# Norm factors in the input blocks, raw queries asked for two steps ahead, values copied inside DRAM to one block per column group and loaded whole

## The chip, the cores and the metric

The kernel runs on one core of one Trainium2 chip. A core has five engines that run side by side and wait for one another by semaphores: TensorE (PE in the profile; its weight loads are listed apart as PEld), VectorE (DVE), ScalarE (ACT), GpSimd (POOL) and SyncE (SP). Here SP does nothing but issue transfers (DMAs), and nearly all of the kernel's transfers stand in that one queue. TensorE writes its results to PSUM, which has eight banks of 128x512 float32 values, and ACT and DVE read them from there.

The metric is the device time of one execution in microseconds (us); lower is better.

## The reference

`DEPTH` is 1, so only the first layer is computed: 2-D neighbourhood attention with 16 heads of 64 on a grid of 32 rows by 64 columns, a SiLU gate and a residual, between two RMSNorms. Everything is float32.

```python
S, D, H, HD = 2048, 1024, 16, 64                  # 32 rows x 64 columns
h = rmsnorm(x, norm_0)                            # x * rsqrt(mean(x*x) + eps) * norm_0
q, k, v, gate = split(h @ w_in_0, 4)              # (2048 x 1024) @ (1024 x 4096)
for every row r and every block of 16 query columns:
    keys   = 8 rows around r x 32 columns around the block
    s = q @ keys.T / 8 + bias(rpb_0)              # only the 8 x 16 keys of the query's own
    o = softmax(where(valid, s, -1e30)) @ v       #   neighbourhood are valid
x = x + (o * silu(gate)) @ w_out_0
return rmsnorm(x, norm_f)
```

## The kernel before

A float32 product is made of three TensorE passes over operands that are split into a high and a low part: high x high, high x low, low x high. A split takes one ACT copy (the high part) and one DVE subtraction (the low part). `split_to` does this for inputs, `split_q` for queries, `split_og` for the attention's result, `use_item` for weights.

The first RMSNorm is not applied to x before the projection. The factor per feature, `norm_0` (`g0`, read through `gain`), is multiplied in when an input block is split. The factor per token, 1/rms, is computed while the first projections run (`stats`), and multiplied into the projection's result. For q, k and gate, whose results lie features by tokens, it is first spread over the partitions: `diagonal(c)` (four small DVE operations, an ACT copy and a DVE subtraction) and `spread_rstd(c)` (two matmuls, one ACT copy) give `rb[c]`, a 128x512 tile for the 512 tokens of chunk c. `evac` then multiplies a PSUM bank by `rb[c]` on DVE (L326 for k, L328 for q and gate), and `out_` does it on GpSimd (L439). For values, `evac_v` multiplies by a column of `rt` on ACT.

The work runs in three stages.

- `stage_one` (chunks 0 and 1, 1024 tokens): the values, then q, k and gate of all eight head pairs by a scheme of seven block products in place of eight (`seven_products`, a Strassen-Winograd form). Twelve units (four times k, q, g) have seven products each, in the order 1, 6, 2, 7, 5, 4, 3; a product is twelve matmuls of 128x128 by 128x512. Some products add into a bank in which an earlier product still stands until DVE has read it (`add`, `out_`). Operands of coming products are formed six products ahead (`ahead`).
- `stage_two` (chunks 2 and 3): the values of these tokens, then three more units.
- The attention loop, 66 iterations of which 64 have a pair (head pair p, token block T of eight grid rows, half of the four column groups C). Iteration i runs, in this order on TensorE: `feed`, some 20 matmuls of what is left (first `projections`, 36 groups of 24 matmuls for chunks 2 and 3, then `outputs`, the product with `w_out`); `turns(i-2)`, the transposes of the probabilities, which ACT and DVE copy out of PSUM into `pta`; `scores(i)`, then DVE adds bias and mask (L970) and ACT takes the exponentials (L973); `values(i-2)`, probabilities times values. `feed(n, calm)` does not stop within `calm` matmuls of the last evacuation.

All of q, k (high and low part), gate and v pass through DRAM (`qd`, `k_hi`, `k_lo`, `sgd`, `vd`) between projection and attention. `vd` holds the values by grid row (r within a group of four, column c, group g). A value tile `vt` for one column group is loaded by four transfers, one for each r (`load_v`, `rows`, L920), since only then the partitions are contiguous in DRAM; that makes 32 blocks x 4 column groups x 4 transfers.

The order of the work is written out by hand, engine by engine. A clock that counts matmuls (`due`) triggers what `store(key, lag, f)` and `later_loads` have put off by `lag` matmuls. `begin(i)` asks for loads: in an even iteration the keys of the next block (lag 0 and 2), then the biases of a new head pair (4 and 6), the gate (7); in every iteration i > 0 the value tiles of pair i-1 (eight transfers from lag 1 on). `middle(i)`, after 45% of the iteration's feed, splits in even iterations the queries that this same iteration's `scores` need, and asks for the raw queries of the next block. In an even iteration in which p or the kind of block changes, `bias` also puts six operations on GpSimd (L945). `split_og(n)` (two ACT copies and two DVE subtractions, L1103 and L1104) is called from `ahead(k)` inside `outputs`, whenever tile n is due within one turn and was loaded long enough ago, whatever the iteration.

Engines take their instructions strictly in this order, so an instruction that waits holds up everything behind it on its engine. Of a pool with n buffers, the next tile waits until a buffer is released by all who read it.

Of the kernel before, what the change touches and what calls it, by code (L numbers as in the profile page):

```python
# [10 lines left out]
F32 = mybir.dt.float32  # L11
# [59 lines left out]
def build(ctx, tc, x, xr, xt, wg, rpb, w_out, n0, nf, masks, out):  # L71
# [7 lines left out]
    vd = [dram.tile([4, 4, GW, 8, 128], F32, name=f"vd{u}") for u in range(2)]  # L79
    ogd = [dram.tile([128, 4, NP, 128], F32, name=f"ogd{T}") for T in range(4)]  # L80
# [71 lines left out]
    def split_x(a, b, t, tiles=None):  # L152
        h, l = tiles or (xs([128, 512], F32R, "hh"), xs([128, 512], F32R, "hl"))
        hh[a, b], hl[a, b] = h, l
        nc.scalar.activation(h, t, AF.Copy, scale=g0[:, a:a + 1])
        nc.vector.scalar_tensor_tensor(l, t, g0[:, a:a + 1], h.bitcast(F32), op0=OP.mult, op1=OP.subtract)

    def use_item(it):
# [3 lines left out]
        if kind == "x":  # L162
            split_x(a, b, t, (hh[a, b], hl[a, b]))
# [125 lines left out]
    pending = []  # L289
# [23 lines left out]
    def flush(c):  # L313
        if c not in rb:
            if c not in dgs:
                diagonal(c)
            spread_rstd(c)
        for e in [e for e in pending if e[0] == c]:
            pending.remove(e)
            e[1]()  # L320

    def evac(kind, hp, c, p, then=None):
        state["event"] = clock[0]
        tmp = ev([128, 512], F32, "tmp")
        if kind == "k":
            nc.vector.tensor_tensor(tmp, p, rb[c], OP.mult)  # L326
        else:
            nc.vector.tensor_tensor(blocked(tmp), tiled(p), tiled(rb[c]), OP.mult)  # L328
# [5 lines left out]
    def give(kind, hp, c, tmp):  # L334
        while sum(e[1][0] in "kqg" for e in later) > 1:
            later.pop(0)[2]()
        s = slice(c * 512, c * 512 + 512)
        if kind == "g":
            sg = ev([128, 512], F32, "sg")
            nc.scalar.activation(sg, tmp, AF.Tanh, scale=0.5)  # L340
            nc.vector.scalar_tensor_tensor(sg, sg, 1.0, tmp, op0=OP.add, op1=OP.mult)
            written.add(("g", hp, c))
            store(("g", hp, c), 12, lambda: nc.sync.dma_start(sgd[hp][:, s], sg))
            return
        written.add((kind, hp, c))
        if kind == "q":
            store(("q", hp, c), 12, lambda: nc.sync.dma_start(qd[hp][:, s], tmp))
# [3 lines left out]
        nc.scalar.activation(hi, tmp, AF.Copy)  # L351
        nc.vector.tensor_tensor(lo, tmp, hi.bitcast(F32), OP.subtract)
# [22 lines left out]
    def evac_v(u, t, p):  # L375
        v = ev([128, 512], F32, "v")
        nc.scalar.activation(v, p, AF.Copy, scale=rt[:, t:t + 1])
# [10 lines left out]
    def seven_products(us, c0, X1, also):  # L388
# [45 lines left out]
        def out_(n, a, c, P, u, then):  # L434
            kind, j = us[n]
            tmp = ev([128, 512], F32, "tmp")
            lay, of = (lambda t: t, lambda t: t) if kind == "k" else (blocked, tiled)
            nc.vector.tensor_tensor(lay(tmp), of(B[n, P]), of(u), OP.add)  # L438
            nc.gpsimd.tensor_tensor(lay(tmp), lay(tmp), of(rb[c]), OP.mult)  # L439
# [16 lines left out]
        def run():  # L456
            then = []
            for i, (n, P) in enumerate(seq):
# [7 lines left out]
                elif P == 2:  # L466
                    evac(kind, 2 * j, c0, B[n, 2], then)
# [901 lines left out]
```

## Time and profile before

| | us |
|---|---|
| median of 3 runs | 1103.4 (1100.61 to 1104.03) |
| the profiled execution | 1102.79 |
| its span, first to last instruction | 1101.0 |
| PE busy | 1080.7 |
| DVE busy | 732.7 |
| ACT busy | 531.5 |
| POOL busy | 378.5 |

The profile is one execution; its span is 1.8 us shorter than the time that was measured for that same execution. Times in views of the trace count from the span's start. Stage one reaches to about 326 us, stage two to about 462 us, the attention loop to about 1046 us; the rest is the end of the output product.

A row of the view by stretches gives the length of the stretch, then for each engine its busy time and number of instructions, the granted TensorE clock (1.00 is full speed) and the busy share and rate of the DMA engines. A row of the timeline gives start, duration, engine, source line, operation and tiles, and in brackets how long the engine had idled and what ended that. A row of the groups gives line, engine, operation, tiles and shape, count, then total busy time in us and the mean of one in ns.

### The profile page before, as it was taken

To read this page: it belongs to the slowest core of one execution; us is meant where nothing else is said; L and a number is where in the kernel's file an instruction comes from. 1 tells how busy PE (TensorE), PEld (TensorE's weight loads), DVE (VectorE), ACT (ScalarE), POOL (GpSimd) and SP (SyncE) were. 2 spreads that over 40 slices of the span, in tenths; PEclk is the share of its full clock that TensorE was granted. 3 is DMA by queue.
4 is the path that set the end of the run, shared out by engine and by line. 5 is a ranking of instruction groups with operands and counts; after the bars stand their busy time and mean duration, and the time that the engine had idled before them with its cause. 6 is when DMAs were issued, how large, how long until landed. Compare 5 with 4: busy or idle time off the path is not lost.

```text
span 1101.0 us, 22543 instructions
## 1 busy us (share of the span) xinstructions
PE 1080.7 (98%) x7657; PEld 883.6 (80%) x7657; DVE 732.7 (67%) x1663; ACT 531.5 (48%) x1336; POOL 378.5 (34%) x483
## 2 busy tenths in 40 slices
PE   9999999999999999999999999999999999999997
PEld 6888888888888888877888888888877888887885
DVE  5376778788777337575665766665777777776644
ACT  7545343343344433255554554564556555555422
POOL 0000312222130001245445444424447666675200
PEclk9999999999999999998999999999999999999999
DMA  8633545454574235587767878687979797887452
GB/s 307 209 96 105 185 132 181 143 173 112 166 216 138 80 89 157 195 263 232 233 193 241 251 223 230 211 268 222 259 237 286 228 288 225 252 274 211 152 153 77
DMA packets 142962, 217.29 MB, mean 197 GB/s; under 512 B 18048, under 2 KB 65408, under 8 KB 142848
## 3 DMA queue, kind: packets, MB, share of 16 engines
q1 hardware_dynamic: 142704, 215.58, 64.6%
q8 instruction: 62, 1.02, 0.4%
q14 instruction: 52, 0.43, 0.1%
q10 hardware_dynamic: 144, 0.26, 0.1%
HBM read 157.05 MB, written 58.72 MB: 196 GB/s over the span
## 4 chain that ended last, share of the span: by engine, by line
PE 88%; DVE 5%; DMA 3%; issue 2%; ACT 1%; POOL 1%; SPq 0%; DVEq 0%; POOLq 0%
PE pp L421 24%; PE pv L534 16%; PE o L1031 7%; PE s L963 6%; PE pp L369 6%; PE pp L367 6%; PE pp L365 5%; PE po L1227 5%; PE po L1223 4%; PE po L1225 4%; PE ph L986 4%; ACT x L973 1%; PE zp L1242 1%; DVE gl L1104 1%; DMA sgt<-sgd 0%
## 5 line engine op out<-in xcount | busy, mean ns | idle before, releaser
L981 POOL TENSOR_SCALAR x<-x,st 128x360 f32<-128x360 f32 (+5 forms) x256 | 143.1, 579 | 239.1 <-DVE st L979 157.1
L439 POOL TENSOR_TENSOR tmp<-tmp,rb 128x512 f32<-128x512 f32 x45 | 73.5, 1634 | 399.2 <-DVE tmp L438 358.4
L973 ACT ACTIVATE x<-x,st 128x360 f32<-128x360 f32 (+5 forms) x256 | 151.8, 594 | 56.4 <-DVE st L970 56.4
L421 PE MATMUL pp<-h,f 128*128 128x512 f32 x480 | 155.4, 389 | 0.0
L945 POOL TENSOR_TENSOR em<-e,mk 128x480 f32<-128x480 f32 (+5 forms) x160 | 140.8, 915 | 5.0 <-DVE st L970 5.0
L421 PE MATMUL pp<-t,f 128*128 128x512 f32 x540 | 129.8, 389 | 0.1
L970 DVE CUSTOM_DVE_ANT_0 x<-s,em 128x360 f32<-128x360 f32 (+5 forms) x256 | 123.8, 538 | 5.1 <-PE s L963 2.0
L421 PEld LDWEIGHTS pp<-t,f 128*128 128x128 f32 x540 | 101.3, 188 | 21.5 <-DVE u L432 0.6
L369 PE MATMUL pp<-h,w 128*128 128x512 f32 x288 | 115.9, 403 | 0.0
L367 PE MATMUL pp<-l,w 128*128 128x512 f32 x288 | 114.2, 397 | 0.0
L365 PE MATMUL pp<-h,w 128*128 128x512 f32 x288 | 113.6, 394 | 0.0
L1010 ACT ACTIVATE pta<-ph 96x256 f32<-96x256 f32 (+1 forms) x224 | 58.8, 333 | 105.8 <-PE ph L986 105.8
L1031 PEld LDWEIGHTS o<-pta,vt 96*64 96x64 f32 (+2 forms) x1792 | 86.0, 139 | 24.2 <-DVE pta L1011 10.2
L421 PEld LDWEIGHTS pp<-h,f 128*128 128x128 f32 x480 | 90.1, 188 | 18.8
L1031 PE MATMUL o<-pta,vt 96*64 96x128 f32 (+4 forms) x1792 | 95.2, 258 | 7.5 <-DVE pta L1011 4.6
L1227 PE MATMUL po<-wol,gh 128*128 128x512 f32 x252 | 101.4, 403 | 0.0
L1223 PE MATMUL po<-woh,gh 128*128 128x512 f32 x252 | 100.0, 397 | 0.0
L1225 PE MATMUL po<-woh,gl 128*128 128x512 f32 x252 | 99.7, 395 | 0.0
L1011 DVE COPY pta<-ph 128x384 f32<-128x384 f32 (+3 forms) x128 | 60.5, 513 | 51.5 <-PE ph L986 51.2
L421 PE MATMUL pp<-l,f 128*128 128x512 f32 x240 | 93.4, 389 | 0.0
L534 PE MATMUL pv<-wh,h 128*128 128x512 f32 x256 | 88.1, 390 | 0.0
L534 PE MATMUL pv<-wh,l 128*128 128x512 f32 x256 | 88.0, 389 | 0.0
(136 smaller groups left out, 1951.1 us busy)
## 6 DMA issues: line engine op xcount, KB each, us to landing
raw<-in_wg_dram SPq DMA_DIRECT2D x126, 256.0 KB
e<-in_rpb_dram SPq DMA_DIRECT2D x54, 240.0 KB
vt<-vd SPq DMA_DIRECT2D x256, 48.0 KB
row<-in_xr_dram SPq DMA_DIRECT2D x32, 256.0 KB
vd<-v SPq DMA_DIRECT2D x32, 256.0 KB
k_hi<-hi SPq DMA_DIRECT2D x32, 256.0 KB
k_lo<-lo SPq DMA_DIRECT2D x32, 256.0 KB
qd<-tmp SPq DMA_DIRECT2D x32, 256.0 KB
```

What stands on the lines that cost most here:

```text
L365: nc.tensor.matmul(p, wh[w, b][:, cols], hh[k, c], start=(k == 0), stop=False)
L367: nc.tensor.matmul(p, wh[w, b][:, cols], hl[k, c], start=False, stop=False)
L369: nc.tensor.matmul(p, wl[w, b][:, cols], hh[k, c], start=False, stop=(k == NK - 1))
L421: nc.tensor.matmul(B[n, P], t[:, int(m == 2), c], x[k][int(m == 1)], start=P in (1, 6, 5) and k == 0 and m == 0, stop=k == 3 and m == 2, s ...
L534: nc.tensor.matmul(ps[t], a[:, o], b, start=k == 0 and m == 0, stop=k == NK - 1 and m == 2)
L945: (nc.gpsimd if attending[0] or not s else nc.vector).tensor_tensor(sh(t), E[p, s][:, u0 + 4:u1 + 4, v0 + 8:v1 + 8], sh(MK[0][:, m0:m0 + n ...
L973: nc.scalar.activation(X[i, C][s], X[i, C][s], AF.Exp, bias=st[:, s:s + 1], scale=-1.0, accum_out=st[:, 2 + s:3 + s])
L981: nc.gpsimd.tensor_scalar(X[i, C][s], X[i, C][s], st[:, 4 + s:5 + s], 0.5, op0=OP.mult, op1=OP.mult)
L1031: nc.tensor.matmul(o[s * 64:s * 64 + 64, C * 128 + q0:C * 128 + q0 + nq], vt[C][:k, g - g0_, s * 64:s * 64 + 64], t[:k, at:at + nq], start ...
L1223: nc.tensor.matmul(p, gh, woh[q, j], start=(i == 0), stop=False)
L1225: nc.tensor.matmul(p, gl, woh[q, j], start=False, stop=False)
L1227: nc.tensor.matmul(p, gh, wol[q, j], start=False, stop=(i == NK - 1))
```

## The change

1. **Norm factors in the input blocks.** For chunks 2 and 3 both factors are multiplied into the raw input block by one DVE operation (`normed`) before it is split. The results of stage two and of the attention loop's projections then need no `rb`: `evac` (with `flush` and `pending`) is gone from `projections`, `out_` skips GpSimd, and `give` works on the PSUM bank itself (`psum=True`): ACT copies the high part of k, or takes the tanh of the gate, or copies q, and DVE reads the bank for k and gate. `diagonal(2)`, `diagonal(3)` and `spread_rstd(2)` move from stage two into stage one, where four of the input blocks are also loaded and eight are normed earlier; `spread_rstd(3)` moves to the start of stage two. In exchange the gate is stored in plain order and reordered when it is used (L1045).
2. **Raw queries two steps ahead.** The queries of the next block are split in the middle of the odd iteration before (`middle`), and the raw queries of the block after that are asked for there, into the one buffer of pool `lp`.
3. **Values as one block per column group.** 64 transfers inside DRAM (`copy_v`) copy `vd` to `vc[p, C]`: 32 in stage one (three in each unit from the second), 32 in stage two. A value tile is then one transfer (`load_v`).
4. **Order in the attention loop.** The two value transfers of `begin` come first (lag 0 and 2), then new biases (5 and 8), keys (9 and 13), gate (15). `split_og` gets a condition: in odd iterations after the first quarter of the feed (`quiet`) up to two turns ahead, in even ones only in the second half of the turn just before.

```diff
+    vc = {(p, C): dram.tile([4 * (c1 - c0), 8, 128], F32, name=f"vc{p}_{C}")
+          for p in range(NP) for C, (c0, c1) in enumerate(KEY_COLS)}
...
-    def give(kind, hp, c, tmp):
+    def give(kind, hp, c, t, psum=False):
...
+            if psum:
+                o = ev([128, 512], F32, "q")
+                nc.scalar.activation(blocked(o), tiled(t), AF.Copy)
+                t = o
...
-        nc.scalar.activation(hi, tmp, AF.Copy)
-        nc.vector.tensor_tensor(lo, tmp, hi.bitcast(F32), OP.subtract)
+        nc.scalar.activation(hi, t, AF.Copy)
+        nc.vector.tensor_tensor(lo, t, hi.bitcast(F32), OP.subtract)
...
-            nc.gpsimd.tensor_tensor(lay(tmp), lay(tmp), of(rb[c]), OP.mult)
+            if c0 == 0:
+                nc.gpsimd.tensor_tensor(lay(tmp), lay(tmp), of(rb[c]), OP.mult)
...
+    def normed(f, c, k, t):
+        nc.vector.scalar_tensor_tensor(t, t, gain(f, k), rb[c], op0=OP.mult, op1=OP.mult)
...
+            if m and i in (1, 3, 5):
+                copies(0, 1)
...
+            if (n, i) == (-3, 1):
+                diagonal(2)
+            if (n, i) == (-3, 3):
+                spread_rstd(2)
+            if (n, i) == (-3, 4):
+                diagonal(3)
...
+        norms = {(-2, 3): ("x11", 0), (-2, 5): ("x11", 1), (-1, 0): ("x11", 2), (-1, 1): ("x11", 3),
+                 (-1, 3): ("x21", 0), (-1, 4): ("x21", 1), (-1, 5): ("x21", 2), (-1, 6): ("x21", 3)}
...
-                    split_to(*X2[f][k], x[k], gain(f, k))
+                    normed(f, 3, k, x[k])
+                    split_to(*X2[f][k], x[k], None)
...
-                pending.append((c, lambda kind=kind, hp=2 * j + a, c=c, p=p: evac(kind, hp, c, p)))
-                flush(c)
+                state["event"] = clock[0]
+                give(kind, 2 * j + a, c, p, True)
...
-        return [lambda r=r: rows(r) for r in range(4)]
+        def block():
+            VT[p, T, C] = t = vp([128, 4, 128], F32, "vt")
+            nc.sync.dma_start(t[:4 * (c1 - c0), :g1_ - g0_], vc[p, C][:, g0_:g1_])
+
+        return [block]
+
+    def copy_v(p, C, h):
+        must(*[("v", p // 4, t) for t in range(8 * h, 8 * h + 8)])
+        c0, c1 = KEY_COLS[C]
+        g = slice(512 * h, 512 * h + 512)
+        nc.sync.dma_start(vc[p, C].rearrange("(r c) g d -> c r (g d)", r=4)[:, :, g],
+                          vd[p // 4][p % 4].rearrange("r c g d -> c r (g d)")[c0:c1, :, g])
...
-            if n < ready["loaded"] and place[n] <= k + 1 and clock[0] - loaded_at[n] >= 28 and whole(n):
+            near = 2 if quiet[0] else 1 if i >= 4 else 0
+            if n < ready["loaded"] and place[n] <= k + near and clock[0] - loaded_at[n] >= 28 and whole(n):
...
+        if 0 < i <= N:
+            p, T, cs = pairs[i - 1]
+            later_loads(load_v(p, T, cs[0]) + load_v(p, T, cs[1]), 0, 2)
...
-                later_loads([kh, kl], 0, 2)
+                kh, kl = load_k(*nx)
                 if nx[0] != p:
-                    later_loads(load_e(nx[0]), 4, 2)
+                    later_loads(load_e(nx[0]), 5, 3)
+                later_loads([kh, kl], 9, 4)
...
-            later_loads([lambda: load_sg(p, T)], 7, 0)
+            later_loads([lambda: load_sg(p, T)], 15, 0)
...
     def middle(i):
-        if i % 2 or i >= N:
-            return
         m = i // 2
-        if type(QT[order[m]]) is not tuple:
-            split_q(*order[m])
-        if m + 1 < len(order):
-            later_loads([LOADS[m + 1][1]], 1, 0)
+        if i % 2 and m + 1 < len(order):
+            split_q(*order[m + 1])
+        if i == 0 or i % 2 and m + 2 < len(order):
+            later_loads([load_q(*order[m + (2 if i else 1)])], 1, 0)
...
+        quiet[0] = i % 2 == 1 or i >= N
+        feed(a * 0.2)
         middle(i)
         feed(a * 0.55, 8)
+        quiet[0] = i >= N
```

119 lines of the change are left out of this document (54 added, 65 removed).

## The prediction, made before the changed kernel ran

> **What bounds the kernel now.** I read the busy shares first, then the chain of waits for TensorE's pace, then a view by stretches for the places where TensorE falls short of that pace.
>
> ```profile
> span 1101.0 us, 22543 instructions
> PE 1080.7 (98%) x7657; PEld 883.6 (80%) x7657; DVE 732.7 (67%) x1663; ACT 531.5 (48%) x1336; POOL 378.5 (34%) x483
> 97.56 70.73 PE pp L421 x312
> 10.00:462.00 452.00, 451.87 (x1993) 373.68 (x1992) 310.36 (x485) 195.42 (x362) 68.63 (x42) 1.00 0.51 154
> 462.00:486.00 24.00, 24.00 (x117) 19.37 (x117) 17.74 (x30) 10.38 (x23) 8.33 (x7) 1.00 0.89 302
> 486.00:508.00 22.00, 19.02 (x158) 14.97 (x155) 14.34 (x44) 11.59 (x38) 14.77 (x23) 0.84 0.77 229
> 508.00:800.00 292.00, 291.59 (x2829) 237.99 (x2828) 183.95 (x515) 155.11 (x470) 133.58 (x200) 1.00 0.79 234
> 800.00:820.00 20.00, 17.95 (x175) 14.35 (x174) 15.70 (x36) 12.87 (x35) 11.15 (x14) 0.91 0.83 255
> 820.00:845.00 25.00, 23.22 (x251) 19.05 (x250) 19.68 (x48) 14.76 (x43) 14.91 (x20) 0.93 0.82 251
> 845.00:1000.00 155.00, 153.47 (x1518) 125.93 (x1520) 115.50 (x351) 90.46 (x268) 101.40 (x140) 1.00 0.83 252
> 1000.00:1022.00 22.00, 20.36 (x188) 16.64 (x186) 13.92 (x45) 11.80 (x36) 12.38 (x19) 0.92 0.77 231
> 1022.00:1046.00 24.00, 23.68 (x213) 19.27 (x212) 13.73 (x40) 9.48 (x26) 6.98 (x10) 1.00 0.44 133
> ```
>
> TensorE is the bound: busy 1080.7 of 1101.0 us, and 312 matmuls in 70.73 us are 0.227 us each, its pace wherever nothing holds it up. The change adds and removes no matmul, so it can only win what TensorE loses to waits. Up to 462 us that is 0.13 us in 452. In the attention loop each stretch loses its idle time (length minus PE busy) and the part of the clock that was not granted. 486 to 508: 2.98 + 22 x 0.16 = 6.5. 800 to 845: 3.83 + 20 x 0.09 + 25 x 0.07 = 7.4. 1000 to 1022: 1.64 + 22 x 0.08 = 3.4. The rest, 0.41 + 1.53 + 0.32 = 2.3. Together **19.6 us is the ceiling** of any gain; I take the end after 1046 us as unchanged.
>
> What stands behind the three large losses? TensorE's waits and the work that ended them:
>
> ```profile
> 493.68 0.39 PE L963 MATMUL s<-kt,ql 64*128 64x264 f32 x2 [0.25 <-DVE ql L499]
> 495.54 0.43 PE L963 MATMUL s<-kt,qh 64*128 64x352 f32 x1 [1.47 <-DVE tmp L326]
> 497.15 0.95 PE L963 MATMUL s<-kt,qh 64*128 64x352 f32 x3 [1.18 <-ACT pta L1010]
> 492.90 0.72 DVE L499 SCALAR_TENSOR_TENSOR ql<-qr,qh 128x512 fp32r<-128x512 f32 x1 [1.69 <-ACT qh L498]
> 494.80 0.68 DVE L326 TENSOR_TENSOR tmp<-pp,rb 128x512 f32<-128x512 f32 x1
> 805.91 4.72 POOL L945 TENSOR_TENSOR em<-e,mk 128x480 f32<-128x480 f32 x4
> 806.91 1.72 DVE L499 SCALAR_TENSOR_TENSOR ql<-qr,qh 128x512 fp32r<-128x512 f32 x1 [1.13 <-ACT qh L498]
> 808.55 2.63 DVE L1104 TENSOR_TENSOR gl<-ograw,gh 128x512 fp32r<-128x512 f32 x2
> 811.83 1.56 PE L1031 MATMUL o<-pta,vt 96*64 96x128 f32 x32 [2.04 <-DVE pta L1011]
> 814.07 0.43 PE pp L369
> L499 DVE SCALAR_TENSOR_TENSOR ql<-qr,qh x32: 677/708/1825, 473.6 to 1012.4; 128x512 fp32r<-128x512 f32 x32
> L1104 DVE TENSOR_TENSOR gl<-ograw,gh x32: 549/684/1779, 808.6 to 1078.3; 128x512 fp32r<-128x512 f32 x30, 128x384 fp32r<-128x384 f32 x2
> ```
>
> At 493 us ACT reaches the query split only after the exponentials, DVE waits 1.69 us for it, and behind it on DVE stands L326, which alone can free a PSUM bank that the scores need. At 808 us the query split and an output split take 1.72 + 2.63 = 4.35 us of DVE where undisturbed ones (medians 0.708 and 0.684) would take 0.71 + 1.37 = 2.1: GpSimd is working on the bias tiles meanwhile. The copy of the transposes stands behind them. Both are even iterations, and the splits stand just ahead of the work that TensorE waits for. After its wait of 2.04 us TensorE runs at 0.43 us a matmul, half pace.
>
> The Trainium skill, page "TensorE: Matmul & The Clock Gate", section "HAM oscillation — how this bites in real kernels", asks for an idle gap over about 3.4 us before the clock falls. This trace differs: waits of 2.04 us and less were followed by half pace, and the measurement decides. By the page the ceiling would be the idle time alone, 0.13 + 10.7 = 10.8 us.
>
> At 1000 us the wait is for a value tile:
>
> ```profile
> 1005.46 5.86 SPq L920 DMA_DIRECT2D vt<-vd  x10
> 1003.28 4.91 DMA sgt<-sgd
> 1010.88 0.92 PE L1031 MATMUL o<-pta,vt 96*64 96x128 f32 x12 [1.64 <-DMA vt<-vd]
> L920 SPq DMA_DIRECT2D vt<-vd x512: 289/379/1847, 480.2 to 1035.9; - x171
> ```
>
> Ten value transfers occupied SP for 5.86 us, behind keys, queries and the gate.
>
> **The change, part by part.** The prices:
>
> ```profile
> L328 DVE TENSOR_TENSOR tmp<-pp,rb 128x512 f32<-128x512 f32 x34 | 23.4, 689 | 37.1 <-PE pp L369 31.2 <-PE pp L421 5.8
> L439 POOL TENSOR_TENSOR tmp<-tmp,rb 128x512 f32<-128x512 f32 x45 | 73.5, 1634 | 399.2 <-DVE tmp L438 358.4 <-DMA raw<-in_wg_dram 12.9 <-DMA qr<-qd 12.0
> L428 ACT ACTIVATE p<-pp 128x512 f32<-128x512 f32 x15 | 9.0, 598 | 44.4 <-PE pp L421 44.4
> L499 DVE SCALAR_TENSOR_TENSOR l<-spot,g,h 128x512 fp32r<-128x512 f32 x6 | 4.4, 748 | 0.1
> L206 DVE TENSOR_SCALAR dg<-ident,rt 128x128 f32<-128x128 f32 x16 | 3.5, 280 | 0.0
> L210 DVE TENSOR_TENSOR dgl<-dg,dgh 128x512 fp32r<-128x512 f32 x4 | 2.8, 692 | 2.8 <-ACT dgh L209 2.8
> 250.00:269.10 19.10, 19.10 (x86) 15.83 (x85) 16.38 (x32) 5.21 (x9) 5.02 (x4) 1.00 0.41 99
> 288.10:307.10 19.00, 19.00 (x86) 15.73 (x85) 14.72 (x20) 6.37 (x11) 4.84 (x4) 1.00 0.50 166
> q1 hardware_dynamic: 142704, 215.58, 64.6%
> ```
>
> *Norm factors, attention loop.* The 36 groups lose one DVE multiplication each, 36 x 0.689 = 24.8 us of DVE, and the 12 of q gain an ACT copy out of PSUM, 12 x 0.598 = 7.2 us of ACT. None of it is TensorE's; it counts through the waits. The link L326 drops out of the chain at 493 us.
>
> *Norm factors, stages one and two.* Nine GpSimd products go, 9 x 1.634 = 14.7 us, and three on DVE. Added on DVE are 16 products of gain and `rb`; the nearest row is L499 on `spot`, 0.748, so 12.0 us. Eight of them are in stage one, with two diagonals of 4 x 0.280 + 0.692 = 1.8 us. Both diagonals fall in the unit of 250 to 269 us: 16.38 + 3.6 = 20.0 of 19.1 us. The unit of 288 to 307 us gets six products: 14.72 + 4.5 = 19.2 of 19.0. DVE is full there, but TensorE needs a sum only after one product in between, 12 x 0.227 = 2.7 us, and an overrun of 0.9 us stays inside that. Bounds: 0, and 4.0 us if all six products are stretched like the worst split (6 x 1.825 = 11.0): 14.72 + 11.0 - 19.0 = 6.7, less the 2.7 of slack. I take 0.5, nearer to nothing. Over both stages DVE is busy 310 of 452 us, and stage two's blocks are needed only two pairs of token tiles later, so 0 there.
>
> *Copies in DRAM.* 16 half-copies per column group: 2 x 8 x 2 x (192 + 256) KB = 14.7 MB. The queue's own row prices a MB at 64.6% x 1101 / 215.58 = 3.3 us of all 16 engines, so 48 us, and double if a move inside DRAM costs twice. They lie between about 116 and 463 us, 347 us in which the DMA share of 0.51 becomes 0.65 or 0.79. TensorE lost nothing at 0.89 (462 to 486 us). 64 issues of 0.38 us are 24 us of SP. I take 0; the bounds are 0 and 1.
>
> *Queries and output splits.* The query split goes to odd iterations, where no new bias tiles occupy GpSimd, a full iteration ahead of its scores. Output splits leave the even iterations but for the last half of a turn. Behind the split on DVE then stands the evacuation of a group, no longer the scores of the same iteration. Of the 6.5 us at 486 to 508 I take 5.0 (bounds 2.5, half, and 6.5), since the weight splits stay; of the 7.4 at 800 to 845, 6.0 (bounds 3 and 7.4), of the scattered 2.3, 1.2 (0.5 and 2.3).
>
> *Values whole, and first.* 512 issues become 128, so 384 x 0.379 = 146 us of SP go, and the two that a pair needs stand ahead of keys, gate and biases. Late next would be gate or keys, and these have more than half an iteration. Of the 3.4 us at 1000 to 1022 I take 2.8 (bounds 0 and 3.4): landing itself takes a few us (4.91 for the gate).
>
> *New waits.* A k or gate bank is now free after ACT and DVE, 0.598 + 0.689 = 1.3 us, and not after 0.689. Of old groups one was seen late (the 1.47 us). I take 1.7 us for one such stall with its slow clock (bounds 0 and 3.5).
>
> Sum: 5.0 + 6.0 + 1.2 + 2.8 = 15.0 gained, 0.5 + 1.7 = 2.2 lost, **12.8 us less**. With the bounds: from 6.0 - 8.5, which is 2.5 more, to 19.6 less. The profiled execution took 1102.79, its span and 1.8 us around it, 0.6 below the median of 1103.4. Against it: 1102.8 - 12.8 = **1090.0 us**.
>
> **Rivals.** *Everything goes*: the ceiling, 1102.8 - 19.6 = 1083. For it: all large losses share one cause. Against: weight splits and GpSimd's stretching remain.
>
> *Only half goes*: whole tiles still land late, since landing and not issuing was the 4.91 us, and splits disturb odd iterations half as much: 3.4 kept, 3 of the 6.0 kept, 12.8 - 2.8 - 3.0 = 7 less, 1096.
>
> *The clock gate by the rule*: had the clock stayed full, only idle time would come back, 2.98 x 0.77 + 3.83 x 0.81 + 1.2 + 1.64 x 0.82 = 7.9, less 2.2: 1097. The row at 814.07 speaks against it. (The rule is that of the section on HAM oscillation of the Trainium skill's page on TensorE named above.)
>
> *It doesn't do what it says*: the queries and output splits are as many as before, and odd iterations have them all now; the same losses reappear there. Gain about 1, 1102.
>
> *Slower: PSUM banks held too long.* Place: the scores' second column group in the iterations that still project (36 x 24 matmuls, 22 to an iteration: 39), which needs the bank of the group that just ended. From the end of that group TensorE has eight matmuls (1.8 us), the transposes and the first scores, about 3 us in all. If ACT with its exponentials comes more than 1.7 us late to the bank, the 1.3 us of the two operations no longer fit. One such stall cost 1.47 us before, without the slow clock. If 12 of the 24 k and gate groups pay it: 12 x 1.47 = 17.6, 1108; if all, 1125. For it: ACT gets all first readings. Against: ACT is busy 155 of 292 us there, and the link through DVE is gone. (The Trainium skill, page "PSUM — Partial Sum Buffer", section "Summary: rules for kernel authors", says to evacuate promptly because the 2 MiB are tight; the 1.47 us agree.)
>
> **How the numbers follow.** Forecast (1086 to 1094) 0.50; everything 0.08; half 0.14; the rule 0.02; same losses elsewhere 0.10; slower 0.16. A measurement of this kernel tells 0.3% from no change, 3.3 us, so faster is below 1100.1: 0.50 + 0.08 + 0.14 + 0.02 = 0.74; same 0.10; slower 0.16. The range runs from the ceiling to the rival of the same losses, with the upper bound of the sum, 1082 to 1106; the slower rival, 0.16, is left out. The forecast's own range is 1086 to 1094.
>
> **What would show it.** In the profile after: PE's idle time and clock in the stretches around 490, 808, 833 and 1010 us; no query split while GpSimd makes bias tiles; 128 value transfers, and no TensorE wait on `vt`; 64 copies with TensorE still at 0.227 us up to 462. I would be wrong if matmuls of stage one wait for DVE's sums, if scores wait for `lo` or `sg`, or if odd iterations show the 2 us waits.

## The result, and the profile after

| | before | after |
|---|---|---|
| median, runs on the same chip | 1103.72 us | 1086.41 us |
| the profiled execution | 1102.79 us | 1086.36 us |
| its span | 1101.0 us | 1084.5 us |

The ratio is 0.9845, with a 95% interval from 0.9821 to 0.9870: the changed kernel is faster, by about 17 us. The prediction was 1090.0 us (1082 to 1106). The busy shares of the profile after, from the page:

```profile
span 1084.5 us, 21929 instructions
PE 1071.1 (99%) x7657; PEld 877.1 (81%) x7657; DVE 703.2 (65%) x1644; ACT 531.2 (49%) x1345; POOL 357.9 (33%) x474
```

The same stages as before the change, in the view by stretches:

```profile
10.00:462.00 452.00, 451.65 (x1991) 373.25 (x1990) 314.98 (x497) 191.27 (x360) 58.94 (x36) 1.00 0.61 185
462.00:484.00 22.00, 22.00 (x105) 17.89 (x104) 16.72 (x27) 6.54 (x13) 3.44 (x4) 1.00 0.93 316
484.00:506.00 22.00, 20.77 (x181) 16.61 (x180) 14.26 (x50) 16.52 (x51) 15.40 (x24) 1.00 0.78 247
506.00:790.00 284.00, 284.00 (x2806) 233.22 (x2805) 157.77 (x481) 158.70 (x477) 131.00 (x198) 1.00 0.77 241
790.00:835.00 45.00, 44.89 (x453) 36.27 (x452) 33.31 (x88) 29.76 (x85) 28.46 (x38) 1.00 0.95 303
835.00:985.00 150.00, 148.49 (x1480) 121.25 (x1480) 109.06 (x343) 86.72 (x257) 95.50 (x136) 1.00 0.80 252
985.00:1028.50 43.50, 42.96 (x421) 35.12 (x416) 28.88 (x84) 21.02 (x61) 18.81 (x29) 1.00 0.55 174
```

TensorE's idle time plus the clock not granted was 6.5 us around 490, 7.4 at 800 to 845 and 3.4 at 1000 to 1022. It is now 1.2, 0.1 and 0.5, and the clock is 1.00 in every stretch of the loop. Up to 462 us nothing has changed: 0.35 us idle in 452, with a DMA share of 0.61 where it was 0.51. Of the ceiling of 19.6 us, 16.5 were won in the span. What is left is mostly the 1.5 us between 835 and 985. TensorE's longest waits in the loop after the change (total, number, longest, in us):

```profile
PE o L1056 <- DVE pta L1036: 1.0, 3, 0.3
PE s L988 <- DVE lo L342: 0.9, 1, 0.9
PE s L988 <- ACT pta L1035: 0.9, 3, 0.4
```

There is no wait on `vt` any more, and no single wait of the loop reaches 1 us. The second row is the wait that the prediction named for k and gate banks. 128 value transfers and 64 copies are in the trace, as foreseen.

### The profile page after: what moved, and what is told of

It reads as the page before. It is cut to its first block, busy times and chain, and to the rows that moved or that the text cites. A ratio compares the mean times of both kernels' runs of the same rounds, so it can differ in the third digit from the quotient of the medians.

```text
span 1084.5 us, 21929 instructions
## 1 busy us (share of the span) xinstructions
PE 1071.1 (99%) x7657; PEld 877.1 (81%) x7657; DVE 703.2 (65%) x1644; ACT 531.2 (49%) x1345; POOL 357.9 (33%) x474
## 4 chain that ended last, share of the span: by engine, by line
PE 92%; DVE 3%; DMA 1%; ACT 1%; issue 1%; SPq 0%; POOL 0%; ACTq 0%; DVEq 0%; POOLq 0%
PE pp L411 23%; PE pv L531 16%; PE o L1056 8%; PE s L988 6%; PE pp L359 6%; PE pp L357 6%; PE pp L355 6%; PE po L1254 6%; PE po L1252 5%; PE po L1250 5%; PE ph L1011 5%; PE zp L1269 1%; DMA k_hi<-hi 1%; DMA land<-in_xt_dram 0%; DVE f L394 0%
## 5 line engine op out<-in xcount | busy, mean ns | idle before, releaser
L970 POOL TENSOR_TENSOR em<-e,mk 128x480 f32<-128x480 f32 (+5 forms) x160 | 136.3, 886 | 138.3 <-DMA raw<-in_xt_dram 135.0
L430 POOL TENSOR_TENSOR tmp<-tmp,rb 128x512 f32<-128x512 f32 x36 | 58.9, 1637 | 270.6 <-DVE tmp L428 223.7
L1056 PEld LDWEIGHTS o<-pta,vt 96*64 96x64 f32 (+2 forms) x1792 | 83.6, 137 | 17.2 <-issue 10.2
L1056 PE MATMUL o<-pta,vt 96*64 96x128 f32 (+4 forms) x1792 | 92.3, 254 | 1.4 <-DVE pta L1036 1.0
```

The lines of the kernel that those rows point to most:

```text
L970: (nc.gpsimd if attending[0] or not s else nc.vector).tensor_tensor(sh(t), E[p, s][:, u0 + 4:u1 + 4, v0 + 8:v1 + 8], sh(MK[0][:, m0:m0 + n ...
L1056: nc.tensor.matmul(o[s * 64:s * 64 + 64, C * 128 + q0:C * 128 + q0 + nq], vt[C][:k, g - g0_, s * 64:s * 64 + 64], t[:k, at:at + nq], start ...
```

## The experiments

All ratios are to the kernel before on the same chip. The kernels ran on several chips, on which the median of the kernel before was 1101.1 to 1103.7 us, so a difference of 1 or 2 us between medians of two kernels can be the chip's. Three parts are told apart: *norm* (norm factors in the input blocks), *values* (blocks, copies and load order) and *splits* (the places of query and output splits).

| kernel | norm | values | query split | output splits | median, us | ratio | interval |
|---|---|---|---|---|---|---|---|
| norm_only | new | old | old | old | 1101.36 | 0.9967 | 0.9948 to 0.9986 |
| values_only | old | new | old | old | 1099.61 | 0.9980 | 0.9966 to 0.9995 |
| schedule_only | old | new | new | new | 1092.89 | 0.9899 | 0.9876 to 0.9922 |
| old_values_and_order | new | old | new | new | 1102.91 | 1.0002 | 0.9985 to 1.0018 |
| old_both_splits | new | new | old | old | 1088.13 | 0.9878 | 0.9859 to 0.9896 |
| old_query_place | new | new | old | new | 1090.23 | 0.9875 | 0.9853 to 0.9898 |
| old_output_split | new | new | new | old | 1082.87 | 0.9805 | 0.9783 to 0.9828 |
| the change | new | new | new | new | 1086.41 | 0.9845 | 0.9821 to 0.9870 |

### Norm factors alone

The kernel before with part 1 of the change, nothing else; its edits in the loop:

```diff
-                pending.append((c, lambda kind=kind, hp=2 * j + a, c=c, p=p: evac(kind, hp, c, p)))
-                flush(c)
+                state["event"] = clock[0]
+                give(kind, 2 * j + a, c, p, True)
```

> The kernel before with the norm factors moved into the input blocks, and nothing else of the change. My theory (each part takes away its own waits): the multiplication L326 drops out ahead of the scores (1.47 us and its slow clock), the query split and the output splits stay in the even iterations and the values stay late: 1099 to 1102 us, with the losses at 800 to 845 and 1000 to 1022 still there. Rival (the load on DVE is the cause, and 24.8 us less of it in the loop is most of the gain): 1090 us or less.

1101.36 us: the theory, not the rival. Its rows by stretches and TensorE's waits:

```profile
484.00:506.00 22.00, 19.98 (x176) 15.91 (x175) 14.71 (x50) 15.62 (x50) 15.76 (x24) 1.00 0.82 251
790.00:835.00 45.00, 41.74 (x422) 33.57 (x418) 34.37 (x83) 29.23 (x83) 24.08 (x32) 1.00 0.85 258
835.00:985.00 150.00, 144.07 (x1413) 118.05 (x1413) 107.60 (x322) 83.87 (x247) 94.98 (x130) 0.99 0.85 250
```

```profile
PE o L1049 <- DMA vt<-vd: 5.0, 4, 2.5
PE o L1049 <- DVE pta L1029: 4.5, 6, 1.4
PE o L1049 <- ACT qh L495: 2.9, 2, 1.6
```

Around 490 us the loss falls from 6.5 to 2.0 us, with the query split where it was. So it was the multiplication L326 in that chain that cost most, not the query split; the next experiment shows it from the other side. But 835 to 985 now loses 5.9 us idle where the kernel before lost 1.5 in 845 to 1000, and waits on `vt` are 5.0 us where they were 1.9. The third row is `vt` too, since the values don't read `qh` (the view names the last event that it sees): by the updates of semaphores in the trace, TensorE went on 0.2 us after the last transfer of the tile had landed (837.80 and 838.04 us, 910.20 and 910.39). What DVE no longer delays, the value tiles delay.

### The schedule without the norm factors

Parts 2 to 4 on the kernel before; the multiplication behind each group stays. Against the change:

```diff
-                give(kind, 2 * j + a, c, p, True)
+                pending.append((c, lambda kind=kind, hp=2 * j + a, c=c, p=p: evac(kind, hp, c, p)))
+                flush(c)
```

> The kernel before with queries, output splits, value blocks and load order as in the changed kernel, and the norm factors left where they were (a multiplication by DVE behind each group). My theory: 1088 to 1092 us, since the splits have left the even iterations and the values come whole; only waits on the multiplication remain. Rival (load on DVE): 1096 us or more.

1092.89 us, 0.9 above the theory's range and on its side of the rival. The wait that stayed, and the stretch around it:

```profile
PE s L985 <- DVE tmp L328: 1.5, 1, 1.5
484.00:506.00 22.00, 18.62 (x126) 14.01 (x126) 12.62 (x41) 11.97 (x37) 12.36 (x20) 0.77 0.80 249
```

The 1.5 us on the multiplication (now L328) are the old 1.47. The whole loss around 490 us is still there, 3.4 idle and 22 x 0.23 = 5.1 of clock, although the query split is no longer in that chain. So the norm part is worth 6.5 us (1092.89 - 1086.41; 6.0 by the ratios) once the rest is there, and 3.6 us (0.33% of 1103) by itself.

### The value part undone

```diff
-        return [block]
+        return [lambda r=r: rows(r) for r in range(4)]
...
-                    later_loads(load_e(nx[0]), 5, 3)
-                later_loads([kh, kl], 9, 4)
+                later_loads([kh, kl], 0, 2)
```

(with the old lags of bias, values and gate, and no copies)

> The changed kernel with the whole part on values undone: four transfers for each column group, no copies inside DRAM, and the old order of keys, values, rows of the bias and gate. With old_load_order (whole blocks in the old order: 1089.4 us) and old_value_loads (four transfers in the new order: 1133.2, where the gate was issued last and landed up to 7.1 us late) it completes the square. Theory now (blocks and order belong together, and the old pair is a consistent one too): the loss at 1000 to 1022 comes back and a few waits on vt with it, each 2 us or more with its slow stretch behind it, 1089 to 1094 us. Rival (whole blocks are worth the 46.8 us that the run in the new order lost, in any order): 1110 us or more.

1102.91 us, between the two: the whole gain is gone, though norm factors and splits are as changed. The profiled execution was the fastest of them, 1099.43 us; TensorE's waits in it:

```profile
PE o L1060 <- DMA vt<-vd: 4.0, 4, 1.4
PE o L1060 <- DMA e<-in_rpb_dram: 2.6, 1, 2.6
PE o L1060 <- ACT x L1002: 2.5, 2, 1.4
```

Neither `e` nor `x` is anything that the values still need there, and in each of these waits TensorE went on 0.1 to 0.3 us after the last transfer of a value tile had landed, so they are `vt` as well: 9.1 us of waits, in iterations 3, 40, 41, 59 and 61, and half pace behind those of iteration 3. Is the value part then what all of the gain consists of?

### The value part alone

Part 3 and the order of the loads on the kernel before, with this in `middle` and the old rule for the output splits:

```diff
-            later_loads([LOADS[m + 1][1]], 1, 0)
+            later_loads([load_q(*order[m + 1])], 1, 0)
```

> The kernel before with the whole part on values (copies inside DRAM, whole blocks, the new order of the loads) and nothing else: norm factors, query split and output splits stay. Undoing this part alone cost 16.5 us (1102.9 against 1086.4), the whole gain, where the prediction had it at 2.8. Theory now (late values stood behind the late copies of the transposes in the same iterations, so each part alone wins little and only both win): DVE's waits at 490, 808 and 833 are still there, 1097 to 1101 us. Rival (values were most of the loss all along, and the rest of the change adds little): 1090 us or less. In between, at 1091 to 1096, the parts share it.

1099.61 us. The rows of its profiled execution (1095.80 us, among the fastest of this kernel):

```profile
484.00:506.00 22.00, 18.44 (x124) 13.59 (x123) 12.81 (x42) 11.48 (x35) 12.99 (x20) 0.77 0.79 238
790.00:835.00 45.00, 41.84 (x441) 34.06 (x440) 36.50 (x85) 28.12 (x80) 26.54 (x34) 1.00 0.91 293
```

```profile
PE o L1053 <- DVE pta L1033: 4.6, 5, 2.0
PE s L985 <- DVE tmp L328: 1.3, 1, 1.3
```

No wait on `vt`, and DVE's waits at 490 and 790 to 835 all in place (3.6 idle and 22 x 0.23 = 5.1 of clock in the first row). So the parts don't add. By ratio, norm alone wins 0.33% and values alone 0.20%, together (old_both_splits) 1.22%. `values` of one iteration needs the copies of the transposes *and* the value tile. With one of them mended the other is what TensorE waits for, in nearly the same places: 490 to 510 and 790 to 845 us.

The theory had the late values already there in the kernel before, hidden behind the late copies. The traces don't bear that out. A tile is there when the semaphores of its transfers have had their last updates. In the kernel before, the tiles of iterations 2, 3, 40 and 41 were there 8.1, 4.7, 1.4 and 1.8 us before TensorE had done the scores and could begin the values; in old_values_and_order they came 1.6, 4.5, 1.8 and 2.9 us after that moment. From iteration 38 to 40 the tiles take nearly the same time in both kernels, 20.9 and 20.4 us, while TensorE took 21.7 us before and takes 17.7 now. The transfers there keep a pace of their own, and what TensorE lost had given them their lead. Iterations 2 and 3 have one more cause: in old_values_and_order SP stands still for 4.8 us until the query split frees the one buffer of pool `lp` for the raw queries, and seven of the eight value transfers of iteration 1 stand behind. Asking for the queries early thus delays the values when these take eight issues. In the kernel before no such wait is seen.

### Blocks or order?

Two kernels undo one half of the value part each. In the first the eight transfers stand where the two blocks stood (lag 0 to 3.5), in the second the blocks keep the old order (values at lag 1 and 7, gate at 7):

```diff
-        return [block]
+        return [lambda r=r: rows(r) for r in range(4)]
...
-            later_loads(load_v(p, T, cs[0]) + load_v(p, T, cs[1]), 0, 2)
+            later_loads(load_v(p, T, cs[0]) + load_v(p, T, cs[1]), 0, 0.5)
```

```diff
-                later_loads([kh, kl], 9, 4)
+                later_loads([kh, kl], 0, 2)
...
-            later_loads(load_v(p, T, cs[0]) + load_v(p, T, cs[1]), 0, 2)
+            later_loads(load_v(p, T, cs[0]) + load_v(p, T, cs[1]), 1, 6)
```

> The changed kernel with the values loaded as before, by four transfers for each column group out of the first layout, but in the new order (ahead of keys and gate); the copies inside DRAM are gone. My theory (issuing is what made values late; the copies cost nothing): the stages up to 462 us stay as they are, and a part of the loss at 1000 to 1022 is back, 1087 to 1090 us. Rival A (the order alone mends it): 1086 to 1087. Rival B (14.7 MB of copies cost something that the four transfers do not): under 1085.5 us.

> The changed kernel with whole value blocks but with the old order of the loads (keys first, values one to seven matmuls later, gate after seven). My theory (fewer issues are what counts): 1086 to 1087.5 us, no wait on vt over 0.5 us. Rival (a block behind two key loads lands late, since landing takes some 4 us): waits on vt of 1 to 3 us and 1088 to 1092 us.

The first took 1133.2 us (ratio 1.0267, 1.0240 to 1.0295), outside everything expected. DVE's wait, and the timeline of one such place:

```profile
DVE og L1074 <- DMA sgt<-sgd: 51.9, 17, 7.1
```

```profile
842.91 0.44 SPq L956 DMA_DIRECT2D sgt<-sgd  x1
843.44 6.83 SPq L942 DMA_DIRECT2D vt<-vd  x8
850.05 0.69 DVE L1074 TENSOR_TENSOR og<-o,sgt 128x512 f32<-128x512 f32 x1 [5.88 <-DMA sgt<-sgd]
```

What is late here is the gate, which the new order puts last, and DVE stands still for 5.88 us with the copies of the next transposes behind it. Eight issues occupied SP for 6.83 us, 0.85 each. Of the 32 gate loads 17 were waited for; after the change none is. So the new order bears only blocks that take one issue.

The second took 1089.43 us (0.9875, 0.9851 to 0.9898), the rival's range, but with a single wait:

```profile
PE o L1056 <- DMA vt<-vc: 2.0, 1, 2.0
```

Of the four combinations (1086.4, 1089.4, 1102.9, 1133.2), blocks are worth 13.5 us in the old order and 46.8 in the new one; the new order is worth 3.0 us with blocks and costs 30.3 without. Up to 462 us the copies cost nothing that can be seen: of 452 us TensorE is busy 451.65 in norm_only without them and in the change with them, 451.87 in the kernel before without them and in values_only with them.

### The query split in its old place

```diff
-        if i % 2 and m + 1 < len(order):
-            split_q(*order[m + 1])
+        if i % 2 or i >= N:
+            return
+        if type(QT[order[m]]) is not tuple:
+            split_q(*order[m])
```

> The changed kernel with the query split back in the middle of the even iteration, half an iteration ahead of its scores, and the raw queries asked for one step ahead. My theory: the loss at 486 to 508 comes back in part and that at 800 to 845 by half, 1090 to 1094 us, with waits of the scores on ql and of the values on pta in even iterations. Rival (with the norm factors gone DVE has room, and the place of the split does not matter): 1086 to 1088 us.

1090.23 us, 3.8 above the change (3.3 by the ratios): the theory's time, but only a part of its places. TensorE waits 3.0 us for `pta` on DVE in three places (longest 1.3) and 1.7 for ACT's; the scores' wait on `ql` is only 0.3 us, and 484 to 506 us loses 1.2 us as in the change, so nothing came back there.

### The output splits by the old rule

```diff
-            near = 2 if quiet[0] else 1 if i >= 4 else 0
-            if n < ready["loaded"] and place[n] <= k + near and clock[0] - loaded_at[n] >= 28 and whole(n):
+            if n < ready["loaded"] and place[n] <= k + 1 and clock[0] - loaded_at[n] >= 28 and whole(n):
```

> The changed kernel with the old rule for the output splits (one turn ahead, in any iteration). My theory: where a split meets GpSimd's bias tiles its two differences take 2.6 us and not 1.4, and the pta copy behind them is late: 1088 to 1091 us. Rival (the query split alone was what made DVE late): 1086 to 1087 us.

1082.87 us, 3.5 us *faster* than the change (4.4 by the ratios): both theory and rival fall. The stretching was real and, with the query split gone from there, did not matter. Two timelines of iteration 44 show why, first the change, then the old rule:

```profile
851.59 0.80 DVE L1182 SCALAR_TENSOR_TENSOR st<-st 128x1 f32<-128x1 f32 x1
852.81 0.75 DVE L1191 SCALAR_TENSOR_TENSOR y<-y,st,acc 128x512 f32<-128x512 f32 x1
853.27 0.91 PE L1011 MATMUL ph<-ident,x 64*96 64x64 f32 x24
854.20 0.63 ACT L1164 ACTIVATE xr<-y 128x512 f32<-128x512 f32 x1 [0.60 <-DVE y L1161]
854.83 0.96 ACT L1035 ACTIVATE pta<-ph 96x256 f32<-96x256 f32 x4
855.40 0.71 PE L988 MATMUL s<-kt,qh 64*128 64x480 f32 x3 [0.45 <-ACT pta L1035]
```

```profile
853.54 1.97 DVE L1129 TENSOR_TENSOR gl<-ograw,gh 128x512 fp32r<-128x512 f32 x2
854.31 0.91 PE L1011 MATMUL ph<-ident,x 64*96 64x64 f32 x24
854.98 0.98 ACT L1035 ACTIVATE pta<-ph 96x256 f32<-96x256 f32 x4 [0.34 <-PE ph L1011]
855.60 0.69 PE L988 MATMUL s<-kt,qh 64*128 64x480 f32 x4
```

`split_og` sets `state["event"]`, and `feed(n, 8)` does not stop within eight matmuls of an event. With the old rule a split late in the iteration puts more of the output product ahead of the transposes: 26 matmuls and not 21 in this iteration, by a count of the trace. The transposes start 1.04 us later, ACT is ready for its copies before they are (it waits 0.34 us for them), and no time is lost, since those matmuls are due anyway. In the change the split isn't there; what delays DVE is the chain of small operations that finishes a row tile (`finish`, L1177 to L1191), which is no event. The delay reaches the scores by way of ACT: its square L1164 waits for DVE's sum L1161 behind that chain, its copies stand behind the square, and the scores wait for them. The new rule's other losses of half a microsecond or more lie in the odd iterations 51, 53 and 61, where output split, query split and work of `finish` now meet ahead of the copies. Iteration 61, where the same square waits for DVE:

```profile
989.69 1.30 DVE L1129 TENSOR_TENSOR gl<-ograw,gh 128x512 fp32r<-128x512 f32 x2 [1.60 <-ACT gh L1128]
990.90 1.81 DVE L1191 SCALAR_TENSOR_TENSOR y<-y,st,acc 128x512 f32<-128x512 f32 x1
...
993.34 0.63 ACT L1164 ACTIVATE xr<-y 128x512 f32<-128x512 f32 x1 [2.03 <-DVE y L1161]
...
994.39 0.56 PE L988 MATMUL s<-kt,qh 64*128 64x288 f32 x3 [0.23 <-ACT pta L1035]
```

Where it was aimed, the rule does help a little; the rows of the old rule for 790 to 835 and 835 to 985:

```profile
790.00:835.00 45.00, 44.55 (x451) 36.14 (x450) 34.35 (x89) 29.79 (x85) 28.97 (x37) 1.00 0.96 306
835.00:985.00 150.00, 150.00 (x1529) 123.58 (x1527) 116.67 (x352) 88.53 (x263) 99.04 (x140) 1.00 0.83 258
```

The first row is that of the old rule with 0.45 us idle, where the change has 0.11; in the second the change loses 1.51 and the old rule nothing. Counted by the length of each iteration, less 0.227 us for each matmul of its feed, the change loses 0.87 us in iteration 44, 0.41 in 48, 1.09 in 51, 0.52 in 53 and 0.68 in 61 against the old rule, 3.6 us in all, and gains 0.3 in 40 and 41. The effect of the rule as a whole is measured; that the event is what makes the difference in iteration 44 is read from the code and the two timelines. Whether `finish` should set the event too was not tried.

### Both splits in their old places

The two edits above together.

> The changed kernel with both splits as before: the query split in the even iteration's middle and the old rule for the output splits. Alone, the first cost 3.8 us and the second won 3.5. Theory now (what counts is how many splits of 0.7 us or more meet in one iteration, not whether GpSimd stretches them): both together in the even iterations pile up as they did before the change at 800 to 845, 1090 to 1095 us, more than the sum. Rival (the two add up): 1086 to 1087.5 us.

1088.13 us, between the two. By the medians the query split's new place is worth 5.3 us with the old output rule (1088.13 - 1082.87) and 3.8 with the new one; TensorE waits five times for `pta` on DVE, 4.7 us in all, longest 1.8. That is more than the sum of 0.3 by 1.4 us, which the medians of two chips don't settle. The traces show a small pile-up in one place: iteration 40 loses 1.85 us more than in the change, and some 0.2 with either split alone in its old place. There the query split (1.59 us) and the output split (2.63) stand on DVE one behind the other, and the copies behind both. Alone each is stretched as much (1.60 us in old_query_place, 2.47 in old_output_split) and costs little, so there it counts that two meet, as the theory has it.

### The price of a wait

```diff
+            if C == cs[0]:
+                for _ in range(EXTRA.get(i, 0)):
+                    nc.vector.tensor_tensor(accs[0], accs[0], accs[0], OP.max)
```

> The changed kernel with 1, 2, 3, 4, 5, 6, 8, 10 and 14 extra DVE operations of 0.69 us (a tile's maximum with itself, which changes nothing of the output) ahead of the first copy of the transposes in nine iterations without losses. It prices a wait and what follows it. My theory: DVE has about 0.4 us of slack there, so the waits are some 0.3, 1.0, 1.7, 2.4, 3.1, 3.8, 5.1, 6.5 and 9.3 us; from a wait of about 2 us on the next matmuls run at half pace (0.43 us) for 1 to 2 us. Rival (the clock only falls after a gap over 3.4 us): 0.227 us right after the waits of 1.7 to 3.1 us, and half pace from the sixth step on.

The sixth step and what followed:

```profile
669.04 2.83 PE L1061 MATMUL o<-pta,vt 96*64 96x128 f32 x32 [3.68 <-DVE pta L1041]
...
672.40 0.63 PE L357 MATMUL pp<-h,w 128*128 128x512 f32 x1
672.82 0.63 PE L359 MATMUL pp<-l,w 128*128 128x512 f32 x1
```

The starts of successive matmuls are the pace: 0.23 us apart at full clock, 0.43 here. The ladder alone does not decide, as it has no step between 1.3 and 3.7 us. Steps one to five cost 0.2, 0.2, 1.5, 0.6 and 1.4 us, mostly far less than the 0.3 to 3.1 expected, so the slack that the copies have differs from place to place; the sixth waited 3.7 where I had 3.8. No step up to the fifth (longest wait 1.29 us) was followed by half pace. The rival falls by the kernel before, which ran at half pace after waits of 2.04 us (the row at 814.07 in the prediction) and of 1.64 us (the row at 1010.88). But the theory's "about 2 us" falls as well: in values_only a wait of 2.04 us was followed by full pace. The stretches around these two waits, first the kernel before, then values_only with its wait:

```profile
1007.94:1011.35 3.41, 1.77 (x30) 1.50 (x29) 2.12 (x9) 2.47 (x9) 3.41 (x6) 1.00 0.52 162
1011.35:1014.77 3.42, 3.42 (x15) 2.73 (x12) 1.38 (x2) 0.40 (x1) 2.46 (x3) 0.50 0.45 129
1014.77:1018.18 3.41, 3.41 (x24) 2.55 (x25) 0.82 (x3) 0.72 (x2) 1.03 (x2) 1.00 0.69 171
```

```profile
811.96 1.56 PE L1053 MATMUL o<-pta,vt 96*64 96x128 f32 x32 [2.04 <-DVE pta L1033]
808.11:811.53 3.42, 1.80 (x28) 1.19 (x24) 3.42 (x6) 0.98 (x4) 2.65 (x3) 1.00 0.60 159
811.53:814.94 3.41, 2.98 (x39) 2.66 (x40) 2.92 (x11) 2.09 (x7) 2.39 (x4) 1.00 1.08 308
```

The borders of these stretches are not chosen freely. In the records of the granted clock, every change in the 14 traces lies a whole number of steps of 3.41 us after the trace's first one, and the clock was then 1.00 or 0.50 for whole steps. So a wait counts by what of it falls into one step: the 1.64 us of the kernel before lie in one step (3.41 - 1.77) and the next has 0.50; the 2.04 us of values_only are cut into 1.62 and 0.43, and the clock stays. Between 440 and 1045 us of all 14 traces, each of the 16 full-clock steps with 1.63 us of idle or more was followed by 0.50; of those with 1.0 to 1.62 us some were, and none with less. Why some of these and not others was not tried. The half clock lasted two steps after the 3.68 us (667.56 to 674.39) and one after a wait of 2.49 us in norm_only (1009.99 to 1013.40). For the 3.68 us it cost 1.3 us in the values (2.83 and not 1.56) and 1.2 in the group behind.

So the clock gate is dearer here than the rule quoted in the prediction. (That rule is in the Trainium skill, page "TensorE: Matmul & The Clock Gate", section "HAM oscillation — how this bites in real kernels"; its 3.4 us of idle time don't agree with the 1.64 and 2.04 us of the kernel before.)

### A PSUM bank less

```diff
-    banks = ctx.enter_context(tc.tile_pool(name="banks", bufs=8, space=PSUM))
+    banks = ctx.enter_context(tc.tile_pool(name="banks", bufs=7, space=PSUM))
```

> The changed kernel with seven PSUM banks in place of eight. It brings every wait for a bank one bank closer, and shows how near the slower rival was (a bank of a k or gate group held 1.3 us and not 0.69). If the margin is as thin as the rival had it: stalls of 1 to 2 us in a dozen iterations or more that project, 1100 us or more. My theory: the release is seldom late, and only a few iterations stall: under 1095 us.

1102.09 us (0.9995, 0.9979 to 1.0011), above my bound: the condition with which the slower rival was to be told is met. The scores of iteration 19 now last 1.94 us and not 1.33, their first four matmuls 1.29 and not 0.69:

```profile
640.01 1.29 PE L988 MATMUL s<-kt,qh 64*128 64x480 f32 x4
```

By the lengths of the iterations, 14 odd ones between 19 and 47 lose 0.6 us each and most other odd ones 0.2 to 0.5, some 13 of the 19.4 us by which the span of this profiled execution (1103.9) is longer than the change's; iteration 3 loses 1.9 more to half clock. Each loss at a bank is far below the 1.47 us of the rival's sum, and it comes in iterations of the output product too, so it is not the bank of a k or gate group alone. With eight banks one wait of 0.9 us is left. The margin is one bank, no more; how much of it the longer hold takes, this run doesn't say.

### A later start of the transposes

```diff
-        feed(a * 0.55, 8)
+        feed(a * 0.55, 14 if i in (2, 38, 40, 41) else 8)
```

(on old_output_split)

> The changed kernel with the old rule for the output splits (1082.9 us) and, in iterations 2, 38, 40 and 41, which alone still lose something there, up to 14 and not 8 matmuls of projection or output between the last evacuation and the transposes. Theory: 6 matmuls, 1.4 us, are about what the scores wait for in iteration 2 (0.8 us and the half us behind it) and in 41, so 1 to 2 us less: 1081 to 1082 us. Rival (what the iteration borrows comes off the next, which is then late instead): 1083 us or more.

1082.60 us (0.9828, 0.9809 to 0.9847) against 1082.87: no difference that can be told, and so neither the 1 to 2 us of the theory nor the loss of the rival. The two fastest kernels of the study are this one and old_output_split, and both beat the change by about 3.5 us in the median.

## Why the prediction was right, and where it was not

The sum was 12.8 us against 16.5 in the span; the measured time lies in the forecast's own range, near its lower end. The direction and the places were right, the causes in good part not.

- **What bounds it, and the ceiling.** Right. TensorE's idle time and clock in four stretches held the whole of what could be won, and 16.5 of 19.6 us came back there.
- **Around 490 us, 5.0 of 6.5.** 5.3 came back, so the size was right. I booked it under the splits. norm_only brings 4.5 of it with the splits in their old places, and schedule_only, with the splits in their new places, brings none: the link L326 was the cause, which the prediction named and gave no price.
- **800 to 845, 6.0 of 7.4.** 7.3 came back, more than taken. The query splits did what was foreseen: none is stretched any more, they take 0.692 us in the median and 0.755 at most, where the worst took 1.825. The query split's new place was worth 3.8 to 5.3 us over the loop by the medians; the new rule for output splits lost 3.5. The failed step is "Output splits leave the even iterations but for the last half of a turn", counted toward the 6.0: I took the 4.35 us of DVE for the price, and overlooked that `split_og` itself holds the transposes back, while `finish`, which it now meets in the odd iterations, does not.
- **Values, 2.8 of 3.4.** The stretch lost 0.5 us and not 3.4, as taken. But undoing the part costs 16.5 us. The failed step is the sum itself: I gave each stretch to the one wait that ended it and added. With the copies in time, the value tiles of the old loading are waited for 9.1 us in iterations 3, 40, 41, 59 and 61. The same tiles were ahead of TensorE in the kernel before, in iteration 3 by 4.7 us and in 40 and 41 by 1.4 and 1.8; winning the other losses uses up that lead, and the raw queries ahead of them in the queue take 4.8 us more at iterations 2 and 3. The question "what is late next" I answered with gate or keys; it would have been the value tiles, had the change not moved them as well.
- **Stage one, 0.5, and copies, 0.** 451.87 busy before and 451.65 after: 0.2 us, all of it from the norm factors, since norm_only has 451.65 and values_only 451.87. TensorE is at 22.00 of 22 us with a DMA share of 0.93.
- **New waits, 1.7.** One, of 0.9 us, and without a slow clock behind it. Right in kind, half the size.
- **The rivals.** *Everything goes* (1083) wasn't reached by the change, but by old_output_split with 1082.9. *Only half* and *it doesn't do what it says* are out as a whole; of the second a small piece is true, for odd iterations 51, 53 and 61 lose some 2 us. *The clock gate by the rule* is out by the half pace after 1.64 and 2.04 us in the kernel before. *Slower by PSUM banks* did not come, though seven banks give 1102: the price of one stall was too high, the number of places too low.

## What to carry over

A view of waits shows the one that ended last, not how far ahead the next one was: before pricing parts that each take away one wait, ask by how much the other work is ahead once all these waits are gone (here leads of 1.4 to 8.1 us were used up, and 0.33% and 0.20% alone made 1.22% together). Where the order of the work is planned, count what the planner does at an operation, not only how long it lasts: a split that pushes the next stage back costs nothing while a filler is there. And a wait of 1 to 2 us can cost its own length or, with a step of half clock behind it, some 1.7 us more (half of 3.41, an estimate); which of the two depends here on how it lies in those steps.

## What the runs showed of the hardware

- The granted clock changed only at points 3.41 us apart, between 1.00 and 0.50. It fell after each of the 16 such steps in which TensorE idled 1.63 us or more (a wait of 1.64 us within one step in the kernel before), and not after a wait of 2.04 us that lay in two steps with 1.62 and 0.43 (values_only).
- DVE operations with both inputs in SBUF stretch while GpSimd works on tiles, and one that handles a single element per row is held up too: L1182 took 0.80 us in iteration 44 and has a median of 0.22 us; L1191 took 1.81 us in iteration 61 and 0.75 in iteration 44. (The Trainium skill, page "GPSIMD Engine Reference", section "Specifications", says that the two engines contend for SBUF when a DVE instruction has two SBUF inputs; the trace agrees.)
- An issue of a transfer took 0.85 us in a row of eight (6.83 us at 843.44), where the same line has a median of 0.36 us in that kernel (old_value_loads).
